# Hybrid decoder layer on one core: a first block in another order, square sums in one bank, the first state-space weights in steps, and stores issued by ScalarE

## The chip, the core and the metric

The kernel runs on one NeuronCore of a Trainium2 chip. The time is the device time of one execution in microseconds (us). The core has a matrix engine (TensorE, PE in the profile), VectorE (DVE), ScalarE (ACT), GpSimd (POOL) and SyncE (SP). Each engine works off its own list of instructions in order. SP and ACT also issue the DMAs of their queues, in their place in that list.

## The reference

One decoder layer for 2048 positions of width 1024, all in fp32:

```python
h = rmsnorm(x, norm_w)
u, z_s, q, k, v, z_a = split(h @ w_in, 6)            # 512 columns each
y_s = s5_branch(u, ...) * silu(z_s)                  # state space: 32 groups of 16 channels, a scan over positions
y_a = diff_attention(q, k, v, ...) * silu(z_a)       # 4 heads, two 64-wide maps each, causal
x = x + concat(y_s, y_a) @ w_out
x = x + sigmoid(x @ ple_w_gate) * (p @ ple_w_proj)
```

`rmsnorm` divides each row of x by the root of its mean square. The kernel multiplies x by the weights first and applies that factor to the result, so it needs a sum of squares for each position, but not before the products.

## The kernel before, in words

Every fp32 product is made of three matmuls of rounded parts: high x high, high x low, low x high (`xh`, `xl` of x, `wh`, `wl` of the weights). For each loaded chunk ACT makes the high part and DVE the low part.

**Phase 1**, to about 697 us, is the input projection, with the state-space branch and its gate unit as background work. The 2048 positions are 8 units of 256. The projection has 12 blocks: a half of the positions (4 units) times one of the six groups of 512 columns. Block 0 is u of the second half, block 1 u of the first half; then come k, s, v, q, a of the first half and s, k, v, q, a of the second. A block needs 8 weight chunks (k = 0 to 7); `ws` keeps 8 of them, and a chunk is released in the block's last unit and then replaced by that of the next block. Three raw chunks (`wraw`) can be in flight; ACT's queue loads them. `xs` keeps five units of x, which SP's queue loads.

In block 0 the first two units are computed together (L760): for k = 0 to 7, 12 matmuls for unit 0 and 12 for unit 1, into eight PSUM banks (4 `pmm`, 3 `pss`, 1 `ptr`). The other units of the u blocks are matmuls of line L781, the k, v, q, a blocks of L827. `stg` takes the u results out of PSUM (L791 by DVE, L793 by ACT).

`squares(unit)` (L253, L254) sums the squares of a unit over the partitions by two matmuls with a column of ones and brings the two columns from the bank `ptr` into `rstd` with one DVE instruction. The pool of `ptr` has one buffer, so the next unit's matmuls wait until that instruction is done. `norm(hf)` raises the eight columns of a half to the power -0.5 on POOL (L259), transposes them on PE (L262) and copies them out of PSUM twice by DVE (L264, L265).

The background is a generator, `ssm()`, that the projection loop advances by some steps after each unit. It makes rotary tables (L323 to L331: positions, angles, sine and cosine), the sum `ld` for attention's lambda from four small vectors `lv` (L335, L339), and the state-space parameters. For each four channel groups, `four(q4)` then makes weights: `na` (L539 to L543), matmuls for a residue (L574), `rs` (L577), which goes through memory and comes back as `M` (L578, L582), transposes (L585) into `wa`, and tables `tx`. `four` is itself a generator of four steps; for the first four groups it is run through at once. The loop over the 32 groups multiplies each group's input `U` by `wa` and by `mg` (made of `M`), scans on DVE, and writes `ysb` (L655) to memory (L656).

**Phase 2**, to about 1186 us, is attention with half of the output projection as filler; **phase 3** is the rest. The change touches neither.

The code is a program whose order on each engine is chosen by a scheduler: it takes instructions by priority (their place in the program, shifted for background work) as their inputs become ready in its own estimate. An edit therefore also moves instructions that it does not name.

Of the kernel before, what the change touches and what calls it, by code (L numbers as in the profile page):

```python
# [11 lines left out]
F32 = mybir.dt.float32  # L12
F32R = mybir.dt.float32r
I32 = mybir.dt.int32
AF = mybir.ActivationFunctionType
ALU = mybir.AluOpType
# [3 lines left out]
D = 1024  # L20
# [4 lines left out]
L = 8  # L25
NCH = S // L
H = 4
EPS = 1e-6
# [50 lines left out]
FLAG = 0  # L79
SADV = 400  # L80
SPB = dict(U=2, wa=2, wc=1, mg=1, xa=1)
FILL = [2] * 4 + [1] * 28
# [36 lines left out]
def hymba_kernel(ctx, tc, x_t, p_t, positions, norm_w, w_in, lam_re, lam_im, log_dt, b_re, b_im,  # L119
                 c_re, c_im, ssm_d, glu_w, glu_b, q_norm_w, k_norm_w, lq1, lk1, lq2, lk2,  # L120
                 subln_w, w_out, w_proj, w_gate, out):
    nc = tc.nc
    V, A, G, T = nc.vector, nc.scalar, nc.gpsimd, nc.tensor
# [74 lines left out]
    with ExitStack() as p1:  # L198
# [18 lines left out]
        sums = {}  # L217

        def build_xt(unit, first, whole):
# [27 lines left out]
            return make  # L247

        def squares(unit):

            pp = ps_tr.tile([128, 4, 128], F32, name="ptr")
            for j in range(2):
                T.matmul(pp[:, 0, j:j + 1], lhsT=sums[unit][:, j * 128:j * 128 + 128], rhs=ones, start=True, stop=True)  # L253
            V.tensor_scalar(rstd[:, unit * 2:unit * 2 + 2], pp[:, 0, 0:2], 1.0 / D, EPS, op0=ALU.mult, op1=ALU.add)  # L254

        def norm(hf):

            rs = rstd[:, hf * 8:hf * 8 + 8]
            G.tensor_tensor(rs, rs, negh[:, 0:8], op=ALU.pow)  # L259

            pp = ps_tr.tile([128, 4, 128], F32, name="ptr")
            T.transpose(pp[:8, 0, :], rs, ident)  # L262
            rt = [pt.tile([128, 8, 2, 8], F32, name=n_, bufs=2)[:8].rearrange("a b c d -> a (b c d)") for n_ in ("ra", "rb")]
            V.tensor_copy(rt[0], pp[:8, 0, :])  # L264
            V.tensor_copy(rt[1].rearrange("a (l c) -> a l c", l=L), pp[:8, 0, :].rearrange("a (c l) -> a l c", l=L))  # L265
            nc.sync.dma_start(rs_scr[hf].rearrange("(a q) -> a q", q=128), rt[0])
            nc.sync.dma_start(rl_scr[:, hf * 128:hf * 128 + 128].rearrange("l (a c) -> a l c", c=16),
                              rt[1].rearrange("a (l c) -> a l c", l=L))
# [36 lines left out]
        ws.fill()  # L305
        xs.fill()
        early_ctx.__exit__(None, None, None)
        early = None

# [3 lines left out]
        def ssm():  # L313

            with tc.tile_pool(name="p1s", bufs=1) as sp:
# [4 lines left out]
                pos_i = sp.tile([128, 16], I32, name="pos_i")  # L320
                nc.sync.dma_start(pos_i, positions)
                posT = sp.tile([128, 16], F32, name="posT")
                V.tensor_copy(posT, pos_i)  # L323
# [8 lines left out]

                lv = [sp.tile([128, 64], F32, name=f"lv{i}") for i in range(4)]
                for t_, a_ in zip(lv, (lq1, lk1, lq2, lk2)):
                    nc.sync.dma_start(t_, a_[0].partition_broadcast(128))  # L335
                ld = sp.tile([128, 2], F32, name="ld")
# [32 lines left out]
            with tc.tile_pool(name="ssA", bufs=1) as sp:  # L369
# [51 lines left out]
                k = 1  # L421
# [90 lines left out]
            with tc.tile_pool(name="ssB", bufs=2) as sp:  # L512
# [96 lines left out]
                for _ in four(0, made):  # L609
                    pass  # L610
                mg4 = within(made[0][2])
# [3 lines left out]
                for g in range(NG):  # L615
# [35 lines left out]
                    def behind(g=g, py=py, w=[w_[:, gs] for w_ in wc4], xa=xa):  # L651
# [3 lines left out]
                        A.copy(ysb, py)  # L655
                        nc.sync.dma_start(yg_scr[g].rearrange("l p c -> (l p) c"), ysb)  # L656
                        if g % 8 == 7:
# [81 lines left out]
        for bi, (hf, kind, c0) in enumerate(blocks):  # L739
            leaving = bi == len(blocks) - 1 or blocks[bi + 1][0] != hf  # L740
            for t in range(4):
# [5 lines left out]
                if kind in ("u", "zs"):  # L747
                    if kind == "u" and t == 0:
                        ude = [pg1.tile([128, L, 128], F32, name="stg") for _ in range(4)]
                    if bi == 0 and t < 2:  # L750

                        if t == 0:
                            first = [pool.tile([128, 512], F32, name=nm)[:, :256] for pool, nm, n in
                                     ((ps_mm, "pmm", 4), (ps_ss, "pss", 3), (ps_tr, "ptr", 1)) for _ in range(n)]
                            for k in range(8):
                                w = ws.get(k)
                                for t_ in range(2):
                                    for cb in range(4):
                                        for n, (a_, b_) in enumerate(passes):
                                            T.matmul(first[t_ * 4 + cb], lhsT=w[b_][:, cb * 128:cb * 128 + 128],  # L760
                                                     rhs=xs.get(t_)[a_][:, k, :],
                                                     start=(k == 0 and n == 0), stop=(k == 7 and n == 2))
                        pos_ = first[t * 4:t * 4 + 4]
# [53 lines left out]
                else:  # L817
# [3 lines left out]
                    for j in range(2):  # L821
# [10 lines left out]
                        if kind == "v":  # L832
                            vo = pt.tile([128, 512], F32, name="t2")
                            A.activation(vo, pm, AF.Copy, scale=rstd[:, ti:ti + 1])
                            nc.sync.dma_start(v_scr[rows, :], vo)
                        elif kind == "za":
# [35 lines left out]
                    if kind in ("q", "k"):  # L872
                        hi_s, lo_s = (qh_scr, ql_scr) if kind == "q" else (kh_scr, kl_scr)
                        nc.sync.dma_start(hi_s[:, :, tok:tok + 256].rearrange("h q t -> q h t"), sh_.bitcast(F32))
                        nc.sync.dma_start(lo_s[:, :, tok:tok + 256].rearrange("h q t -> q h t"), sl_.bitcast(F32))
                if kind == "u" and (bi, t) != (1, 3):
                    squares(xseq[xi + t])
                    if last_t:
                        norm(hf)
                if leaving:  # L880
                    xs.release()
# [517 lines left out]
```

## Time and profile before

| | |
|---|---|
| median of three runs | 1454.8 us (1452.43 to 1457.49) |
| the profiled execution | 1451.3 us |
| its span, first to last instruction | 1449.6 us |
| PE busy | 1383.4 us, 95% |
| DVE, ACT, POOL busy | 74%, 53%, 36% |
| mean granted TensorE clock | 0.992 |

PE is busy nearly all the time, so what can be gained or lost is in its idle stretches and in stretches at a lower clock. The views below are read in that order: how much PE idles in each stretch, who ended each wait, and what the releasing engine did before.

### The profile page before, as it was taken

Reading aid. Unit: us, or ns where it says so; the run is one execution under the profiler, and the core shown is the slowest. Engines: PE = TensorE matmul, PEld = TensorE weight load, DVE = VectorE, ACT = ScalarE, POOL = GpSimd, SP = SyncE. Lnnn points to the kernel's source line nnn. Section 1 sums busy time; section 2 is a strip of 40 time slices with the busy share of each in tenths; the row PEclk is TensorE's granted clock in tenths of the full one; section 3 lists DMA queues with packets and bytes.
Section 4 is the critical chain, followed back from the end, with each engine's and each line's share of the span. In section 5 each row is a group of like instructions: output and inputs, shape, how many; then the busy total and the mean of one; then the engine's idle time right before and its main releaser. Section 6 shows DMA issues by size and latency. Waiting matters only on the chain.

```text
span 1449.6 us, 27391 instructions
## 1 busy us (share of the span) xinstructions
PE 1383.4 (95%) x9602; PEld 1270.7 (88%) x9602; DVE 1066.3 (74%) x2527; ACT 767.9 (53%) x1689; POOL 521.3 (36%) x670
## 2 busy tenths in 40 slices
PE   7899899899999999999899999999998999999998
PEld 7898798778798888887699899989898999999998
DVE  8588898799798866675577867777877448666754
ACT  8443345456554555453586777767787523322231
POOL 6632500144000421331144454454434335543440
PEclk9999999999999999999999999999999999999999
DMA  7549756546765386556864653655434365132221
GB/s 248 152 109 293 209 178 191 166 145 191 245 192 165 107 240 186 138 150 203 240 176 121 164 143 117 162 149 142 127 88 161 138 231 227 59 117 81 73 74 59
DMA packets 219410, 230.34 MB, mean 159 GB/s; under 512 B 62712, under 2 KB 168328, under 8 KB 216712
## 3 DMA queue, kind: packets, MB, share of 16 engines
q1 hardware_dynamic: 203144, 199.22, 45.8%
q10 hardware_dynamic: 16128, 29.37, 6.6%
q8 instruction: 75, 1.23, 0.4%
q14 instruction: 63, 0.52, 0.1%
HBM read 152.19 MB, written 84.72 MB: 163 GB/s over the span
## 4 chain that ended last, share of the span: by engine, by line
PE 37%; DVE 5%; ACT 3%; issue 2%; DMA 2%; POOL 1%; SPq 0%; DVEq 0%; ACTq 0%; POOLq 0%
PE pg L1265 11%; PE po L1102 7%; PE pmf L931 6%; PE pss L1066 6%; PE pl L1281 3%; PE ptw L1098 3%; ACT s L1077 2%; DVE wgt L1157 1%; DVE s L1068 1%; PE pm L931 1%; DVE s L1090 1%; DMA wgr<-in_ple_w_gate_dram 1%; DVE wg L1153 0%; DMA yt_scr<-yo 0%; DMA yin<-yt_scr 0%
## 5 line engine op out<-in xcount | busy, mean ns | idle before, releaser
L827 PE MATMUL pmm<-wh,xh 128*128 128x512 f32 x512 | 198.3, 396 | 3.9 <-ACT wh L282 2.8
L827 PE MATMUL pmm<-wl,xh 128*128 128x512 f32 x512 | 200.4, 395 | 0.0
L827 PE MATMUL pmm<-wh,xl 128*128 128x512 f32 x512 | 200.0, 393 | 0.0
L1066 PE MATMUL pss<-ks,qd 128*128 128x512 f32 (+3 forms) x640 | 185.8, 388 | 10.3 <-DVE st L1068 6.3
L1077 ACT ACTIVATE s<-s,st 128x1024 f32<-128x1024 f32 (+4 forms) x192 | 171.7, 899 | 37.9 <-DVE st L1068 33.1
L1265 PE MATMUL pg<-oph,wg 128*128 128x256 f32 x896 | 164.4, 286 | 3.0 <-ACT oph L1238 2.9
L1102 PE MATMUL po<-vt,wt 128*128 128x128 f32 x1088 | 152.7, 276 | 0.8 <-ACT yo L1114 0.7
L1102 PEld LDWEIGHTS po<-vt,wt 128*128 128x128 f32 x1088 | 142.2, 192 | 7.2 <-ACT yo L1114 0.9
L1265 PEld LDWEIGHTS pg<-oph,wg 128*128 128x128 f32 x896 | 141.5, 195 | 3.4 <-ACT oph L1238 3.4
L1068 DVE CUSTOM_DVE_ANT_0 s<-pss,mk,st 128x512 f32<-128x512 f32 (+2 forms) x192 | 121.7, 652 | 24.3 <-PE pss L1066 22.9
L781 PE MATMUL pmm<-xh,wl 128*128 128x256 f32 x448 | 127.2, 287 | 2.7 <-DVE wl L283 2.6
L1265 PE MATMUL pg<-opl,wg 128*128 128x256 f32 x448 | 127.2, 285 | 1.2 <-POOL opl L1239 1.2
L781 PE MATMUL pmm<-xh,wh 128*128 128x256 f32 x448 | 123.0, 288 | 5.3 <-DVE stg L791 1.5
L781 PE MATMUL pmm<-xl,wh 128*128 128x256 f32 x448 | 125.8, 284 | 0.0
L1066 PEld LDWEIGHTS pss<-ks,qd 128*128 128x128 f32 x640 | 100.4, 192 | 22.8 <-DVE st L1068 11.6
L827 PEld LDWEIGHTS pmm<-wh,xh 128*128 128x128 f32 x512 | 96.1, 188 | 25.3 <-ACT wh L282 5.7
L827 PEld LDWEIGHTS pmm<-wl,xh 128*128 128x128 f32 x512 | 96.5, 188 | 19.2 <-DVE wl L283 1.5
L827 PEld LDWEIGHTS pmm<-wh,xl 128*128 128x128 f32 x512 | 96.5, 189 | 18.6
L931 PE MATMUL pmf<-yh,woh 128*128 128x256 f32 x352 | 104.8, 298 | 4.7 <-DVE x L1188 3.8
L1068 DVE CUSTOM_DVE_ANT_0 s<-pss,mk 128x512 f32<-128x512 f32 (+3 forms) x128 | 78.6, 630 | 34.3 <-PE pss L1066 28.6
L931 PE MATMUL pmf<-yh,wol 128*128 128x256 f32 x352 | 99.8, 284 | 0.0
L931 PE MATMUL pmf<-yl,woh 128*128 128x256 f32 x352 | 99.6, 283 | 0.0
(385 smaller groups left out, 3822.6 us busy)
## 6 DMA issues: line engine op xcount, KB each, us to landing
wraw<-in_w_in_dram ACTq DMA_DIRECT2D x96, 256.0 KB
xraw<-in_x_t_dram SPq DMA_DIRECT2D x40, 256.0 KB
tab<-tab_scr SPq DMA_DIRECT2D x64, 136.0 KB
qd<-qh_scr SPq DMA_DIRECT2D x64, 128.0 KB
qd<-ql_scr SPq DMA_DIRECT2D x64, 128.0 KB
xr<-in_x_t_dram SPq DMA_DIRECT2D x32, 256.0 KB
yin<-yt_scr SPq DMA_DIRECT2D x16, 512.0 KB
xp_scr<-xp SPq DMA_DIRECT2D x32, 256.0 KB
```

The lines of the kernel that those rows point to most:

```text
L781: T.matmul(pm, lhsT=w[b_][:, cb * 128:cb * 128 + 128], rhs=xt[a_][:, k, :], start=(k == 0 and n == 0), stop=(k == 7 and n == 2))
L827: T.matmul(pm, lhsT=xt[a_][:, k, j * 128:j * 128 + 128], rhs=w[b_], start=(k == 0 and n == 0), stop=(k == 7 and n == 2))
L931: T.matmul(pm[:, e, :], lhsT=w[k][b_][:, ms], rhs=y[a_][:, k, :], start=(k == 0 and n == 0), stop=(k == 3 and n == 2))
L1066: T.matmul(pss[:, :cl], lhsT=qd[:, e, m, tq], rhs=ks[m][:, c0:c0 + cl], start=e == 0, stop=e == 1)
L1068: V.tensor_tensor_reduce(sr[m][pi][:, o:o + cl], pss[:, :cl], mk[:, end - cl:end], scale=1.0, scalar=3.4e38 if ci == 0 else st[:, 2 * ci - ...
L1077: A.activation(sr[m][pi][:, :cl], sr[m][pi][:, :cl], AF.Exp, bias=st[:, ci + m:ci + m + 1], scale=-1.0, accum_out=st[:, 12 + 2 * pi + m:13 ...
L1090: V.scalar_tensor_tensor(s0, s1, st[:, 11:12], s0, op0=ALU.mult, op1=ALU.add)
L1098: T.transpose(ptw[:, k, :], blocks_[kg + k], ident)
L1102: T.matmul(po[:, 0:128], lhsT=wt[:, k, :], rhs=vt[:, kg + k, :], start=kg + k == 0, stop=kg + k == len(blocks_) - 1)
L1157: V.tensor_tensor(t_, a_, b_, op=ALU.subtract)
L1265: T.matmul(banks[mp][:, e], lhsT=wg[n][k][b_][:, m * 128:m * 128 + 128], rhs=x_[a_][:, k], start=k == 0 and q == 0, stop=k == 3 and q == 2)
L1281: T.matmul(banks[mp][:, e], lhsT=wp[k][b_][:, m * 128:m * 128 + 128], rhs=p_[a_][:, k], start=(k == 0 and q == 0), stop=(k == 1 and q == 2))
```

## The change

There are four edits, and one that goes with each of two.

1. In block 0 the second unit runs two steps behind the first (`UL = 2`): unit 0 with k = 0, 1, then unit 0 with k and unit 1 with k - 2, and at the end unit 1 with k = 6, 7. The third unit's loads are written after the second unit, those of the next two after the third.
2. The square sums of the four units of a half go to one bank, two columns each, with no evacuation between them. `norm` takes all eight columns at once with an ACT copy that scales, adds the epsilon on POOL, and copies the transposed columns out with ACT instead of DVE. The sums of block 0's first two units are written together after its second unit.
3. The first `four` gives a step back to the projection loop after each of its parts, like the later ones. The four loads of `lv` stand ahead of the rotary tables.
4. The stores of `ysb`, of v, and of the high parts of q and k are issued by ACT's queue instead of SP's: 32 + 16 + 16 DMAs.

```diff
@@ squares, norm
+        psq = [None, None]
         def squares(unit):
-            pp = ps_tr.tile([128, 4, 128], F32, name="ptr")
+            hf, u = divmod(unit, 4)
+            if psq[hf] is None:
+                psq[hf] = ps_tr.tile([128, 4, 128], F32, name="ptr")
             for j in range(2):
-                T.matmul(pp[:, 0, j:j + 1], lhsT=sums[unit][:, j * 128:j * 128 + 128], rhs=ones, start=True, stop=True)
-            V.tensor_scalar(rstd[:, unit * 2:unit * 2 + 2], pp[:, 0, 0:2], 1.0 / D, EPS, op0=ALU.mult, op1=ALU.add)
+                T.matmul(psq[hf][:, 0, u * 2 + j:u * 2 + j + 1], lhsT=sums[unit][:, j * 128:j * 128 + 128], rhs=ones,
+                         start=True, stop=True)
         def norm(hf):
             rs = rstd[:, hf * 8:hf * 8 + 8]
+            A.activation(rs, psq[hf][:, 0, 0:8], AF.Copy, scale=1.0 / D)
+            G.tensor_scalar(rs, rs, EPS, None, op0=ALU.add)
             G.tensor_tensor(rs, rs, negh[:, 0:8], op=ALU.pow)
...
-            V.tensor_copy(rt[0], pp[:8, 0, :])
-            V.tensor_copy(rt[1].rearrange("a (l c) -> a l c", l=L), pp[:8, 0, :].rearrange("a (c l) -> a l c", l=L))
+            A.copy(rt[0], pp[:8, 0, :])
+            A.copy(rt[1].rearrange("a (l c) -> a l c", l=L), pp[:8, 0, :].rearrange("a (c l) -> a l c", l=L))
@@ the background's first steps
+                for t_, a_ in zip(lv, (lq1, lk1, lq2, lk2)):
+                    nc.sync.dma_start(t_, a_[0].partition_broadcast(128))
                 posT = sp.tile([128, 16], F32, name="posT")
...
                 for _ in four(0, made):
-                    pass
+                    yield
@@ stores
-                        nc.sync.dma_start(yg_scr[g].rearrange("l p c -> (l p) c"), ysb)
+                        nc.scalar.dma_start(yg_scr[g].rearrange("l p c -> (l p) c"), ysb)
...
-                            nc.sync.dma_start(v_scr[rows, :], vo)
+                            nc.scalar.dma_start(v_scr[rows, :], vo)
...
-                        nc.sync.dma_start(hi_s[:, :, tok:tok + 256].rearrange("h q t -> q h t"), sh_.bitcast(F32))
+                        nc.scalar.dma_start(hi_s[:, :, tok:tok + 256].rearrange("h q t -> q h t"), sh_.bitcast(F32))
@@ block 0
-                            for k in range(8):
+                            for t_, k in [(t_, k_ - UL * t_) for k_ in range(8 + UL) for t_ in range(2) if 0 <= k_ - UL * t_ < 8]:
                                 w = ws.get(k)
...
-                if kind == "u" and (bi, t) != (1, 3):
-                    squares(xseq[xi + t])
+                if kind == "u" and (bi, t) not in ((0, 0), (1, 3)):
+                    for t_ in ((0, 1) if (bi, t) == (0, 1) else (t,)):
+                        squares(xseq[xi + t_])
                     if last_t:
                         norm(hf)
+                if bi == 0 and t == 1:
+                    xs.make(1)
+                if bi == 0 and t == 2:
+                    xs.fill()
```

**The order on PE, in block 1.** These are PE's rows in the first half's u block where square sums stand; `ptr_` is a bank's allocation and `acc_` a unit's sums. Before:

```order
L781 MATMUL pmm_1045<-xh_404,wl_974 128x256
L781 MATMUL pmm_1045<-xl_405,wh_973 128x256
L253 MATMUL ptr_1146<-ones_188,acc_411 128x1 x2
L253 MATMUL ptr_1339<-ones_188,acc_654 128x1 x2
L781 MATMUL pmm_1042<-xh_404,wh_985 128x256
```

and now:

```order
L785 MATMUL pmm_1040<-xl_613,wh_993 128x256
L258 MATMUL ptr_1141<-ones_188,acc_619 128x1 x2
L258 MATMUL ptr_1141<-ones_188,acc_649 128x1 x2
L258 MATMUL ptr_1141<-ones_188,acc_688 128x1 x2
L785 MATMUL pmm_1231<-xh_642,wh_908 128x256
```

Before, the second pair of sums needs a new allocation of the one bank; now three units stand in the same allocation.

**The order on DVE, at the start of block 1.** `wl` are the low parts of block 1's weights; `rpk`, `rpr`, `rpc` are the rotary angles, `xl` parts of later units of x. Before:

```order
L283 SCALAR_TENSOR_TENSOR wl<-wraw,nw,wh 128x512
L171 SCALAR_TENSOR_TENSOR rpr<-rpk,rpr 128x128
L283 SCALAR_TENSOR_TENSOR wl<-wraw,nw,wh 128x512
L172 SCALAR_TENSOR_TENSOR rpr<-rpk,rpr 128x128
L173 TENSOR_SCALAR rpr<-rpr 128x128
L174 SCALAR_TENSOR_TENSOR rpc<-rpr 128x128
L791 COPY stg<-pmm 128x32x8
L175 TENSOR_SCALAR rpc<-rpc 128x128
L254 TENSOR_SCALAR rstd<-ptr 128x2
L224 TENSOR_TENSOR xl<-xraw,xh 128x512
L283 SCALAR_TENSOR_TENSOR wl<-wraw,nw,wh 128x512 x2
```

and now:

```order
L225 TENSOR_TENSOR xl<-xraw,xh 128x512 x3
L795 COPY stg<-pmm 128x32x8
L290 SCALAR_TENSOR_TENSOR wl<-wraw,nw,wh 128x512 x3
L795 COPY stg<-pmm 128x32x8
L290 SCALAR_TENSOR_TENSOR wl<-wraw,nw,wh 128x512 x5
L795 COPY stg<-pmm 128x32x8 x2
L330 CAST posT<-pos_i 128x16
L333 TENSOR_SCALAR ang<-posT 128x16 x8
```

The eight weight chunks now stand together, and the angles come behind them.

**The order on DVE, at the start of the state-space loop.** From the first weights `na` to the residue `rs`, in the change from block 2 to block 3. Before:

```order
L543 TENSOR_TENSOR na<-na,tabt 128x512
L871 SCALAR_TENSOR_TENSOR stg<-ptr,knw,stg 128x4x128
L560 TENSOR_TENSOR tabt<-pt_2055 128x544
L853 TENSOR_TENSOR t_2417<-pmm,qst 128x512
L283 SCALAR_TENSOR_TENSOR wl<-wraw,nw,wh 128x512
L525 TENSOR_TENSOR Ul<-U,Uh 128x256
L847 TENSOR_REDUCE qst<-t_2564 128x8
L562 TENSOR_TENSOR tx<-tx,tabt 128x544
L283 SCALAR_TENSOR_TENSOR wl<-wraw,nw,wh 128x512
...
L560 TENSOR_TENSOR tabt<-pt_2055 128x544
L577 TENSOR_TENSOR rs<-pss,dd 128x64
```

and now:

```order
L547 TENSOR_TENSOR na<-na,tabt 128x512
L865 TENSOR_TENSOR ra<-t_2430,kc 128x128
L866 TENSOR_TENSOR rb<-t_2430,ks 128x128
L290 SCALAR_TENSOR_TENSOR wl<-wraw,nw,wh 128x512
L529 TENSOR_TENSOR Ul<-U,Uh 128x256
L564 TENSOR_TENSOR tabt<-pt_2045 128x544
L867 TENSOR_TENSOR t_2430<-ra,rb 128x8x8
L868 TENSOR_TENSOR t_2430<-ra,rb 128x8x8
L875 SCALAR_TENSOR_TENSOR stg<-ptr,knw,stg 128x4x128
L566 TENSOR_TENSOR tx<-tx,tabt 128x544
L581 TENSOR_TENSOR rs<-pss,dd 128x64
```

There were 12 instructions between the two and are 9, and the piece now starts when all but the last of block 3's weight chunks are done, where it stood ahead of all of them.

## Rows read from the trace of the kernel before

**Rows 1.** Busy time by stretch; columns: engines, PEclk the granted clock, DMA share.

```profile
core 0: us, PE busy (x) PEld busy (x) DVE busy (x) ACT busy (x) POOL busy (x), PEclk, DMA share, GB/s
0.00:200.00 200.00, 179.59 (x1269) 167.96 (x1270) 158.93 (x499) 96.02 (x181) 86.99 (x103) 0.99 0.67 202
200.00:700.00 500.00, 480.17 (x2730) 413.49 (x2729) 384.37 (x870) 256.44 (x565) 106.92 (x125) 1.00 0.61 179
700.00:1450.00 750.00, 723.61 (x5607) 689.29 (x5606) 523.01 (x1160) 415.46 (x944) 327.39 (x442) 0.99 0.43 134
```

**Rows 2.** Waits of PE in 0 to 200 us: total us, times, longest.

```profile
PE pmm L760 <- ACT xh L223: 6.1, 1, 6.1
PE ptr L253 <- DVE rstd L254: 3.5, 1, 3.5
PE pmm L781 <- DVE wl L283: 2.6, 3, 1.1
PE pss L530 <- ACT mgh L524: 1.9, 1, 1.9
PE pmm L781 <- DVE stg L791: 1.5, 1, 1.5
PE pmm L781 <- ACT wh L282: 1.3, 2, 0.9
...
PE pmm L781 <- DVE rpc L175: 1.0, 1, 1.0
PE pss L530 <- ACT wah L524: 0.6, 1, 0.6
```

**Rows 3.** PE's timeline at the end of L760: start, us, instruction, idle before.

```profile
30.76 0.28 PE L760 MATMUL ptr<-xl,wh 128*128 128x256 f32 x1
32.52 0.35 PE L781 MATMUL pmm<-xh,wh 128*128 128x256 f32 x1 [1.48 <-DVE stg L791]
32.71 0.28 PE L781 MATMUL pmm<-xh,wl 128*128 128x256 f32 x1
32.83 0.28 PE L781 MATMUL pmm<-xl,wh 128*128 128x256 f32 x1
```

**Rows 4.** DVE's timeline: the third weight chunk's low part; ahead of the square sums' wait.

```profile
8.30 0.74 DVE L283 SCALAR_TENSOR_TENSOR wl<-wraw,nw,wh 128x512 fp32r<-128x512 f32 x1
...
73.32 0.23 DVE L339 CUSTOM_DVE_ANT_0 lj<-lv,lv 128x64 f32<-128x64 f32 x1 [1.74 <-DMA lv<-in_lambda_k_dram]
...
73.55 0.15 DVE L254 TENSOR_SCALAR rstd<-ptr 128x2 f32<-128x2 f32 x1
```

**Rows 5.** Busy time by stretch, short stretches; columns as in Rows 1.

```profile
56.00:66.00 10.00, 7.33 (x57) 6.62 (x56) 7.12 (x15) 7.27 (x14) 4.83 (x5) 1.00 0.82 234
74.68:78.10 3.42, 3.42 (x19) 3.42 (x18) 2.66 (x5) 1.51 (x4) 3.42 (x5) 0.50 0.72 196
78.10:82.00 3.90, 3.90 (x34) 3.90 (x34) 3.27 (x14) 2.89 (x6) 2.96 (x4) 1.00 0.49 124
160.00:186.00 26.00, 20.32 (x148) 17.92 (x147) 25.46 (x51) 12.98 (x22) 12.35 (x13) 1.00 0.79 235
```

**Rows 6.** POOL's timeline: the power of the first half normalised.

```profile
61.82 1.66 POOL L259 TENSOR_TENSOR rstd<-rstd,negh 128x8 f32<-128x8 f32 x1 [1.43 <-DVE rstd L254]
```

**Rows 7.** PE's timeline at the first residue matmuls.

```profile
160.59 0.51 PE L574 MATMUL pss<-parg,na 128*128 128x16 f32 x4
```

**Rows 8.** The tile `rs`: its instruction, duration ns, first and last start us.

```profile
L577 DVE TENSOR_TENSOR rs<-pss,dd x1: 220/220/220, 167.1 to 167.1; 128x64 f32<-128x64 f32 x1
```

**Rows 9.** The tile `M` in 160 to 180 us, and who waited for it.

```profile
L582 SPq DMA_DIRECT2D M<-r_scr x1: 370/370/370, 172.9 to 172.9; - x1
L524 ACT CAST mgh<-M x1: 617/617/617, 177.7 to 177.7; 128x512 fp32r<-128x512 f32 x1
```

**Rows 10.** A store that ACT issues already: ns min/median/max, first and last start.

```profile
L842 ACTq DMA_DIRECT2D za_scr<-t x16: 326/326/352, 364.4 to 714.0; - x16
```

**Rows 11.** Waits of SP's queue: total us, times, longest.

```profile
SPq L656 <- ACT ysb L655: 20.2, 14, 4.9
```

**Rows 12.** Waits of PE in 200 to 700 us.

```profile
PE pss L530 <- ACT ysb L655: 3.2, 3, 2.6
...
PE pmm L827 <- ACT wh L282: 2.8, 4, 1.4
```

**Rows 13.** Waits of ACT.

```profile
ACT wh L282 <- DMA wraw<-in_w_in_dram: 47.9, 28, 5.8
```

More of the change, by code (lines that the diff above doesn't have):

```diff
@@ L80 @@
 SADV = 400
+UL = 2
 SPB = dict(U=2, wa=2, wc=1, mg=1, xa=1)
@@ L321, in ssm @@
                 nc.sync.dma_start(pos_i, positions)
+                lv = [sp.tile([128, 64], F32, name=f"lv{i}") for i in range(4)]
+                for t_, a_ in zip(lv, (lq1, lk1, lq2, lk2)):
+                    nc.sync.dma_start(t_, a_[0].partition_broadcast(128))
                 posT = sp.tile([128, 16], F32, name="posT")
@@ L331, in ssm @@
                 A.activation(cos_t, c, AF.Sin)
-                lv = [sp.tile([128, 64], F32, name=f"lv{i}") for i in range(4)]
-                for t_, a_ in zip(lv, (lq1, lk1, lq2, lk2)):
-                    nc.sync.dma_start(t_, a_[0].partition_broadcast(128))
                 ld = sp.tile([128, 2], F32, name="ld")
@@ L754, in hymba_kernel @@
                                      ((ps_mm, "pmm", 4), (ps_ss, "pss", 3), (ps_tr, "ptr", 1)) for _ in range(n)]
-                            for k in range(8):
+                            for t_, k in [(t_, k_ - UL * t_) for k_ in range(8 + UL) for t_ in range(2) if 0 <= k_ - UL * t_ < 8]:
                                 w = ws.get(k)
[L757 to L762, printed above, removed]
+                                for cb in range(4):
+                                    for n, (a_, b_) in enumerate(passes):
+                                        T.matmul(first[t_ * 4 + cb], lhsT=w[b_][:, cb * 128:cb * 128 + 128],
+                                                 rhs=xs.get(t_)[a_][:, k, :],
+                                                 start=(k == 0 and n == 0), stop=(k == 7 and n == 2))
                         pos_ = first[t * 4:t * 4 + 4]
@@ L873, in hymba_kernel @@
                         hi_s, lo_s = (qh_scr, ql_scr) if kind == "q" else (kh_scr, kl_scr)
-                        nc.sync.dma_start(hi_s[:, :, tok:tok + 256].rearrange("h q t -> q h t"), sh_.bitcast(F32))
+                        nc.scalar.dma_start(hi_s[:, :, tok:tok + 256].rearrange("h q t -> q h t"), sh_.bitcast(F32))
                         nc.sync.dma_start(lo_s[:, :, tok:tok + 256].rearrange("h q t -> q h t"), sl_.bitcast(F32))
-                if kind == "u" and (bi, t) != (1, 3):
-                    squares(xseq[xi + t])
+                if kind == "u" and (bi, t) not in ((0, 0), (1, 3)):
+                    for t_ in ((0, 1) if (bi, t) == (0, 1) else (t,)):
+                        squares(xseq[xi + t_])
                     if last_t:
                         norm(hf)
+                if bi == 0 and t == 1:
+                    xs.make(1)
+                if bi == 0 and t == 2:
+                    xs.fill()
+                    early_ctx.__exit__(None, None, None)
+                    early = None
                 if leaving:
```

3 lines of the change are left out of this document (removed).

## Prediction

> **What bounds the kernel now.** I read the views in this order: how much PE idles in each stretch, who ended those waits, what the releasing engine did just before, and where PE ran at the lower clock.
>
> PE is the bound nearly everywhere. It idles 20.4 us in the first 200 us, 19.8 in the next 500 and 26.4 in the rest [rows 1], so 1383.4 us of the span are matmuls that the change neither adds to nor takes away. What it can win lies in those gaps. The rest after 700 us is not touched, and of the first 200 us a start of 6.1 us is fixed, because the same first x part ends it before and after [rows 2]. What is left there is 14 us, and the reader should see in [rows 2] how it is split: 3.5 us behind the square sums, 2.6 behind low parts of weights, 1.9 and 0.6 behind the first state-space weights, 1.5 behind `stg`, 1.3 behind high parts, 1.0 behind a rotary angle. Each edit aims at one of these. The profiled execution took 1451.3 us, 3.5 below the median of the runs, so I work against 1451.3 and add 3.5 at the end.
>
> **(a) The first block.** Before, all eight banks of L760 are finished together, and the first matmul of L781 waits 1.48 us for the first `stg` [rows 3]. Now unit 0 ends 24 matmuls ahead of unit 1, 2.9 us at the pace of 0.12 us [rows 3]. That covers the 1.48 us: I take +1.5. The price could be at the other end: the third weight chunk is needed after 24 matmuls instead of 48. From PE's start at 6.1 that is not before 9.0, and its low part is done at 9.04 [rows 4], so nothing to a few hundredths is lost there; were every later chunk late by as much as the order moves it, 2.9 us would go. Bounds -1.4 to +1.5.
>
> **(b) The square sums.** PE waits 3.5 us for `rstd` [rows 2]. DVE's evacuation of the two columns starts at 73.55, directly behind the sum `lj`, which waited 1.74 us for the DMA of `lv` [rows 4]. The evacuation itself lasts 0.15, and it is what stands ahead of it on DVE that costs. With one bank there is no evacuation between units: PE has the three pairs in one run in the order, and the wait has no place left. The four `lv` loads, now ahead of the tables, remove the second cause as well. +3.5.
>
> Behind this wait the granted clock is 0.50, that is 1.2 GHz, from 74.68 to 78.10, and 19 matmuls start in that time. In the next 3.90 us, at 1.00, 34 do, 0.115 us each [rows 5]. At that pace 19 take 2.2 us, so the low clock cost 1.2 us. It fell right behind PE's 3.5 us pause, and the waits of about 1 us left it alone (56 to 66 us: 2.7 us idle in three pieces, granted 1.00 [rows 5]). Without the pause it should stay up: +1.2. The Trainium skill ("TensorE: Matmul & The Clock Gate", Terms) prices such a stretch at its length times the missing share of the clock, which here is an estimate of 1.7 us; the sum would be 0.5 higher by it. I keep 1.2, from matmuls counted at either level. Bounds of (b): 0, if another wait of that length takes its place (a rival below), to +4.7.
>
> **(c) Weights at the change to block 1.** In 56 to 66 us PE idles 2.7 us [rows 5], behind a low part, a high part and an angle (all within the sums of [rows 2]). On DVE the eight low parts now stand in one run, and the angles come after them. The angle's 1.0 goes entirely, since those instructions are moved out of the stretch. The low part's wait should go too; a high part that is late because its load is late stays late (DMA share there is 0.82 [rows 5]). I take +2.0; bounds 0 to +2.7.
>
> **(d) The norm chain.** Instead of one power per half behind finished `rstd`, the chain is ACT copy, POOL add, POOL power, transpose. The power takes 1.66 us [rows 6]; the trace has no such copy or add, so I bound each by 0 and 1.66 and get 1.7 to 5.0 for the three. By the order PE has 49 matmuls (5.9 us at 0.12) between the last sums and the transposes in the first half, and 39 (4.7 us) in the second. So it is covered unless the copy queues on ACT behind a wait for a load: those are 47.9 us in 28 waits, mean 1.7, longest 5.8 [rows 13]. A mean one gives 3.4 to 6.7 against 5.9 and 4.7: I take -0.5; bounds 0 and -4.7, the pause and low clock of (b) again. The DVE copies of the transposed columns go to ACT with nobody waiting closely, 0.
>
> **(e) The first state-space weights.** From the residue matmuls at 160.59 [rows 7] to `rs` at 167.1 [rows 8] and `mgh` done at 178.3 [rows 9] is a chain of 17.7 us. Meanwhile the order gives PE 63 projection matmuls and 16 transposes, and PE idles 5.7 us while DVE is busy 25.5 of 26 [rows 5]. So these took about 12.0 us, 7.2 in the matmuls at 0.115 and 0.3 for each transpose. After, 80 matmuls and 12 transposes stand there: 9.2 + 3.6 = 12.8. The chain has 9 DVE instructions instead of 12 in its first 6.5 us, so three times 0.54 = 1.6 less: 16.1. Idle 3.3 instead of 5.7, a gain of 2.4. But what remains now gathers at one place: the low parts that had let PE wait in small pieces are done before the piece starts, and PE runs up to the first state-space matmul earlier than `mgh` is there. Taking the transposes at twice a matmul, 0.23, PE has 12.0 us, idle is 4.1, a gain of 1.6; one pause of about 4 us, as long as that of (b), can bring back the low clock, -1.2. I take +1.0. Bounds: all 5.7, if the steps spread out cover the chain; and if the chain stays 17.7 with only the 9.2 us of matmuls beside it, 8.5 idle, -2.8. The whole branch begins about 10 us later in PE's order, but it ends well ahead of the end of phase 1 and is background there: 0.
>
> **(f) The stores.** 64 stores go from SP's queue to ACT's. ACT issues one in 0.326 us [rows 10], 21 us in all, on an engine that is busy half of the time. SP waited 20.2 us for `ysb` [rows 11]; nobody stood behind most of it. PE waits 3.2 us for `ysb` and 2.8 for high parts between 200 and 700 us [rows 12]. If a load on SP stood behind a waiting store it now comes sooner, up to +3.2; if weight loads stand behind stores on ACT, as much is lost. Here is a rule against the edit: "DMA: Bandwidth & Descriptors" of the Trainium skill (Issuing engines are not separate DMA queues) says that all issuers share the 16 engines and that issuing from several saves only the issue time. No row here tests it; by it this term would be zero at best. I take 0; bounds -3.2 to +3.2 and a lower one in a rival.
>
> Sum: 1.5 + 4.7 + 2.0 - 0.5 + 1.0 + 0 = 8.7. 1451.3 - 8.7 = 1442.6; with 3.5 for the median 1446.
>
> **Rivals.**
>
> *Everything gains.* (c) is 2.7, (e) 5.7, (f) 3.2, (d) 0: 17.8 us, median 1437. For it speaks that each wait has its cause moved; against it that DMA is busy 0.67 of the first 200 us [rows 1], so loads remain late.
>
> *The gain is paid back at the start of the state-space loop.* PE gets there earlier, and the chain over memory (`rs`, `M`, `mgh`, 11.2 us [rows 8, 9]) is not shorter: (e) at -2.8 with -1.2 of low clock replaces +1.0, and (d) at -1.2: 8.7 - 5.0 - 0.7 = 3.0, median 1452. For it: DVE is full there [rows 5].
>
> *The change doesn't do what it says in the square sums.* The wait moves to the transposes: the copy behind a late load on ACT, (d) -4.7, and (c) at 0 since the cause is the loads: 8.7 - 4.2 - 2.0 = 2.5, median 1452. Against it are the 49 matmuls of cover.
>
> *Slower: stores hold back weight loads.* A store of q or k is 512 KB, 2.2 us at the 235 GB/s of a full stretch [rows 5]. At six block starts (those around k, v and q in both halves) it can now stand ahead of the next block's weight loads in ACT's queue, and ACT already waits 47.9 us for these loads [rows 13]. One store's time per block start costs 13 us against 8.7: median 1459. It decides from 2.2 us of lateness at each: (8.7 + 4.4) / 6, with 4.4 the 0.3% that a measurement can tell from no change. Against it: the loads wait for released chunks as well as for the queue, and PE's waits for high parts are only 2.8 us so far [rows 12].
>
> **How the numbers follow.** Forecast 0.52, everything gains 0.18, paid back 0.16, moved wait 0.05, slower 0.09. Faster by over 0.3% (below 1450.4) is the first two, 0.70; the two at 1452 are within, 0.21; slower (above 1459.2) 0.09. The predicted time is 1446. Below, the range goes to 1437, the likely upper gain. Above, it goes to 1456, past the two at 1452 by the 3.5 us that a run may lie beside its median, and leaves out the slower case and some of each tail. The forecast alone is 1441 to 1450, from (e) and (f).
>
> **What would show it.** (a) no gap at the first L781. (b) no wait behind square sums, and granted 1.00 around 75 us. (c) idle in 56 to 66 us under 1. (d) the transposes of `norm` do not wait for POOL. (e) one wait of 3 to 5 us for `mgh` or `wah` at the first state-space matmul; two would be the paid-back case. (f) PE's waits for `wh` in 200 to 700 us stay at about 3 us; 10 or more would make the prediction wrong on the slow side, and idle in phase 1 down by more than 12 us on the fast side.

## The result, and the profile after

The change takes 1464.25 us (median of 4 runs, 1463.15 to 1466.97) where the kernel before takes 1453.62 in the same group of runs: a ratio of 1.0074, 95% interval 1.0051 to 1.0097. It is 10.6 us slower; I had forecast 1446, and 1437 to 1456 as the range. The profiled execution took 1464.1 us with a span of 1462.4. Later groups of runs were on several chips, on which the kernel before took 1453 to 1459 us; each ratio below is against the kernel before of the same group.

The busy time by stretch, in the columns of [rows 1], shows the same split as there:

```profile
0.00:200.00 200.00, 184.20 (x1317) 173.37 (x1318) 160.67 (x483) 94.44 (x183) 87.19 (x105) 0.99 0.65 204
200.00:700.00 500.00, 475.62 (x2674) 407.92 (x2673) 385.15 (x873) 259.09 (x566) 113.41 (x125) 0.99 0.60 179
700.00:1450.00 750.00, 724.19 (x5566) 691.44 (x5565) 519.59 (x1154) 415.27 (x942) 326.85 (x442) 0.98 0.42 133
```

PE's idle time fell from 20.4 to 15.8 us in the first 200 us, but rose from 19.8 to 24.4 in the next 500. The third row hides its loss: phase 3 begins later, so a stretch of dense work after 1450 us is no longer in it. A better measure is the time between two matmuls that both kernels have. These are the first and last starts of three lines on PE: the projection of the k, v, q, a blocks, attention's scores, and the products of phase 3. Of the kernel before:

```profile
L827 PE MATMUL pmm<-wh,xh x512: 387/389/628, 114.2 to 704.3; 128*128 128x512 f32 x171
L1066 PE MATMUL pss<-ks,qd x640: 222/393/688, 683.9 to 1136.7; 128*128 128x512 f32 x100, 128*128 128x256 f32 x28, 128*128 128x384 f32 x28, 128*128 128x128 f32 x4
L1265 PE MATMUL pg<-oph,wg x896: 280/283/580, 1231.4 to 1442.7; 128*128 128x256 f32 x180
```

and of the change, whose lines stand 4 and 11 further down:

```profile
L831 PE MATMUL pmm<-wh,xh x512: 387/389/763, 106.6 to 706.7; 128*128 128x512 f32 x171
L1077 PE MATMUL pss<-ks,qd x640: 220/393/776, 682.3 to 1144.2; 128*128 128x512 f32 x100, 128*128 128x384 f32 x28, 128*128 128x256 f32 x27, 128*128 128x128 f32 x5
L1276 PE MATMUL pg<-oph,wg x896: 278/283/553, 1243.7 to 1455.8; 128*128 128x256 f32 x180
```

Read them as three clocks. Block 2 starts 7.6 us earlier (106.6 for 114.2). At the end of phase 1 nothing is left of that: the last projection matmul is 2.4 us later, the first score matmul 1.6 earlier. Then the piece from the first score to the first matmul of phase 3, which I call the attention span, takes 561.4 us instead of 547.5. That is 13.9 us more, in a part of the program of which no line was edited. The windows of that span, first of the kernel before, then of the change:

```profile
683.90:1231.40 547.50, 528.05 (x3947) 491.66 (x3946) 394.40 (x1033) 361.42 (x878) 243.85 (x410) 0.99 0.53 160
682.30:1243.70 561.40, 536.76 (x3970) 501.28 (x3968) 395.05 (x1034) 363.90 (x880) 243.89 (x411) 0.98 0.51 157
```

Idle time of PE is 5.2 of the 13.9 us (24.64 for 19.45). The other 8.7 stand in PE's busy time. A part of them is a lower clock: in the change the granted clock is 0.50 from 901 to 908, 976 to 980 and 1113 to 1116 us, each time at a wait of PE of 1.5 to 3.8 us or just behind it. The kernel before has 1.00 from 717 to 1231 us.

PE's waits in the first 200 us, as in [rows 2], say how the early gain came about and where it went:

```profile
PE pmm L764 <- ACT xh L224: 5.5, 1, 5.5
PE pmm L831 <- DVE t L857: 3.9, 1, 3.9
PE pmm L785 <- ACT wh L289: 3.0, 2, 2.3
PE pss L534 <- ACT Uh L528: 2.1, 1, 2.1
PE pmm L785 <- ACT stg L797: 0.5, 1, 0.5
PE pmm L831 <- DVE wl L290: 0.3, 1, 0.3
PE ptr L258 <- DVE qnw L359: 0.3, 1, 0.3
```

The wait of the square sums is 0.3 instead of 3.5. The waits for `stg` ahead of the third unit and for the rotary angle are gone; the 0.5 for `stg` is another wait, at 80 us in block 1. New is the second row: 3.9 us in block 2, at 133 us, for DVE's `t` (L857; L853 before). In short stretches, with the columns of [rows 5], the clock stays up where it had fallen and falls at the new pause. First the change, then two of these stretches in the kernel before:

```profile
56.00:66.00 10.00, 9.27 (x75) 8.77 (x74) 4.13 (x6) 3.50 (x8) 9.13 (x11) 1.00 0.90 266
66.00:90.00 24.00, 23.50 (x193) 23.10 (x194) 13.65 (x49) 9.93 (x19) 9.92 (x13) 1.00 0.44 128
120.00:140.00 20.00, 16.10 (x66) 12.94 (x66) 15.04 (x86) 4.50 (x7) 6.02 (x8) 0.91 1.00 324
```

```profile
66.00:90.00 24.00, 20.53 (x159) 20.37 (x159) 15.95 (x51) 13.59 (x24) 14.44 (x17) 0.93 0.72 201
120.00:140.00 20.00, 19.02 (x84) 15.29 (x83) 17.53 (x95) 5.17 (x8) 4.01 (x5) 1.00 1.05 327
```

ACT's timeline just before that pause shows what is late:

```profile
126.78 0.64 ACT L470 COPY par<-s_bs 64x512 f32<-64x512 f32 x1 [5.98 <-DMA s_bs<-in_ssm_c_re_dram]
127.45 0.65 ACT L471 ACTIVATE par<-s_bs 64x512 f32<-64x512 f32 x1
128.12 0.65 ACT L472 ACTIVATE par<-s_bw 128x512 f32<-128x512 f32 x1
128.68 1.24 ACT L849 ACTIVATE t<-pmm,rstd 128x512 f32<-128x512 f32 x2
```

ACT stood 6 us for a load of the matrix C, and the squares of block 2's first products (L849) stood behind it in ACT's list. The reduction on DVE, the power on POOL and `t` on DVE follow them, and only `t` frees PE's bank. DMA is busy all of that stretch (share 1.00). PE had run ahead of the background work, and the background set the pace. The last matmul of block 2 starts at 158.1 us instead of 160.4, so 2.3 of the 7.6 us are left there.

### The profile page after: what moved, and what is told of

Its sections match the earlier page's. It is cut to its first block, busy times and chain, and to the rows that moved or that the text cites. A ratio compares the mean times of both kernels' runs of the same rounds, so it can differ in the third digit from the quotient of the medians.

```text
span 1462.4 us, 27302 instructions
## 1 busy us (share of the span) xinstructions
PE 1390.3 (95%) x9602; PEld 1278.8 (87%) x9602; DVE 1069.6 (73%) x2515; ACT 770.1 (53%) x1693; POOL 527.5 (36%) x672
## 4 chain that ended last, share of the span: by engine, by line
PE 53%; DMA 17%; DVE 14%; ACT 5%; POOL 5%; issue 4%; SPq 2%; ACTq 0%; DVEq 0%; POOLq 0%
PE pg L1276 11%; PE pmf L942 7%; PE po L1113 7%; PE pss L1077 6%; PE pmm L785 5%; PE pmm L831 4%; DMA wraw<-in_w_in_dram 3%; PE pl L1292 3%; PE ptw L1109 3%; PE pm L942 2%; POOL qst L853 1%; DMA gz<-zs_scr 1%; ACT s L1088 1%; DMA yin<-yt_scr 1%; DMA U<-ug_scr 1%
## 5 line engine op out<-in xcount | busy, mean ns | idle before, releaser
L831 PEld LDWEIGHTS pmm<-wh,xl 128*128 128x128 f32 x512 | 97.1, 190 | 18.2
```

The source lines that it names most:

```text
L831: T.matmul(pm, lhsT=xt[a_][:, k, j * 128:j * 128 + 128], rhs=w[b_], start=(k == 0 and n == 0), stop=(k == 7 and n == 2))
```

## The experiments

After the result I had four theories. **S**: stores on ACT hold back weight loads. **F**: the background, pushed back by four steps, is late. **O**: an edit lets the scheduler order everything behind it anew, phase 2 too, and that order costs the time. **D**: phase 2 loses because what phase 1 hands it comes late.

**Each edit undone alone.** The four kernels are the change with one of its four edits taken back.

```diff
# u_stores: yg_scr, v_scr and hi_s again
-  nc.scalar.dma_start(...)
+  nc.sync.dma_start(...)
# u_four (and the lv loads back behind the tables)
-  for _ in four(0, made): yield
+  for _ in four(0, made): pass
# u_sq: squares() and norm() of the kernel before
# u_blk: UL = 0, loads and sums of the first units as before
```

> The change without its fourth edit: all stores are issued by SP's queue as before. If stores ahead of weight loads in ACT's queue cost the 10 us (theory S), the time falls to that of before or below, 1447 to 1455 us, and the matmuls of the k, v, q, a blocks lose less on the way to the end of phase 1. If the loss is that the scheduler orders everything after an edit anew, phase 2 among it (theory O), the early gain of 6 us stays, the end of phase 1 moves by a few us either way, and phase 2 takes another time than with the change without any store of phase 1 being in it: total between 1445 and 1468.

> The change without its third edit: the first weights are made in one go, and the small vectors are loaded behind the tables, as before. If the background that is pushed back by four steps costs the time (theory F), the end of phase 1 comes 5 to 10 us earlier and the total falls to 1445 to 1455. By theory O the total is anywhere in 1445 to 1468 and phase 2's part of it changes too; by theory S it stays at 1464 within 3.

> The change without its second edit: square sums unit by unit through the one bank, evacuated by DVE. The wait of 3.5 us at the second unit and the low clock behind it may come back, so the early gain shrinks by up to 4.7. By theory O the total is anywhere in 1445 to 1468; by theories S and F it is 1464 to 1469.

> The change without its first edit: the first two units side by side. The gap of 1.5 us ahead of the third unit comes back. By theory O the total is anywhere in 1445 to 1468; by theories S and F it is 1464 to 1467.

Measured: `u_stores` 1.0060 (1.0036 to 1.0084), `u_four` 1.0064 (1.0039 to 1.0089), `u_blk` 1.0066 (1.0040 to 1.0091), `u_sq` 1.0134 (1.0091 to 1.0178). Taking back none of the edits brings the time back. Without the square sums' edit it looks worse still: beside the 1453.6 us of the first group it would be 1473, above what any of the theories allowed, though its interval reaches down to 1467 and so into O's range. S and F fall as they were put: neither the stores alone nor the steps alone are the cause. Each of the four kernels was also ordered anew, so these runs don't price the edits; `r_all_stores` below does that for the stores. The attention spans are 555.8, 560.5, 552.6 and 567.0 us: four other values, though all four kernels have the same code there.

**Phase 2's order exchanged.** Here and below a kernel is held to an order: after the program is written and before it is scheduled, each instruction of an engine gets an edge to the one ahead of it in the wanted list. The edge orders only; it adds no semaphore.

```diff
+ for p, i in pairs_in_the_wanted_order:
+     tc.add_manual_dep(i, p.name, NoSync)
```

`r_p2` is the change with phases 2 and 3 in the order of the kernel before, `x_p2` the kernel before with phases 2 and 3 in the order of the change.

> The change, with phase 2 and 3 held to the order that each engine has in the kernel before; phase 1 stands as in the change. Theory O (the scheduler's new order of phase 2 costs the 10 us lost there): 1464 falls to 1452 to 1457. Rival D (phase 2 loses because what phase 1 hands it comes late): it stays within 3 of 1464.

> The kernel before, with phase 2 and 3 held to the order that they have in the change. Theory O: 8 to 12 us slower than before, 1463 to 1468. Rival D: as before, 1453 to 1457.

Measured: `r_p2` 1.0026 (1.0006 to 1.0046), `x_p2` 1.0073 (1.0048 to 1.0098). The first matmul of scores and of phase 3, in `x_p2` and then in `r_p2`:

```profile
L1066 PE MATMUL pss<-ks,qd x640: 220/393/775, 687.1 to 1150.1; 128*128 128x512 f32 x100, 128*128 128x384 f32 x28, 128*128 128x256 f32 x27, 128*128 128x128 f32 x5
L1265 PE MATMUL pg<-oph,wg x896: 280/283/553, 1249.5 to 1460.6; 128*128 128x256 f32 x180
```

```profile
L1077 PE MATMUL pss<-ks,qd x640: 222/393/687, 695.9 to 1150.2; 128*128 128x512 f32 x100, 128*128 128x256 f32 x28, 128*128 128x384 f32 x28, 128*128 128x128 f32 x4
L1276 PE MATMUL pg<-oph,wg x896: 280/283/416, 1246.0 to 1457.7; 128*128 128x256 f32 x180
```

The attention span goes with the order, whatever stands ahead of it: 562.4 us for the kernel before with the change's order, 550.1 for the change with the order of before (561.4 and 547.5 in their own kernels). Put into the kernel before alone, the order costs 0.73%, 10.6 us, as much as the whole change. On this chip the kernel before took 1458.4 us, so the forecasts, which are times, are read as ratios. Beside the 1453.6 us of the first group `x_p2` would be at 1464.2, within O's range, and `r_p2` at 1457.4: 7 us below the change, where D allowed 3, and just above O's 1452 to 1457. D falls; for phase 2, O holds.

**The early gain in the order of before.** `r_b2_after` is the change with everything written from block 2 on in the order of before, `r_b2_e123` the same with the stores on SP.

> The change, with everything that is written from block 2 on held to the order of the kernel before (the 64 moved stores stand free in ACT's queue). Theory O: the early gain of about 6 us stays and nothing is lost behind it, 6 to 9 us faster than before, 1446 to 1450. Theory S (stores on ACT cost): 1455 or more, though the run without them below is fast. Rival D: 1460 or more.

> The same without the fourth edit: stores on SP's queue, and the order of the kernel before from block 2 on. Theory O: 6 to 9 us faster than before, 1446 to 1450. Against the run above it gives the fourth edit alone: within 3 us by my forecast of zero for it, 8 us or more by theory S.

Measured: 0.9998 (0.9976 to 1.0021) and 0.9987 (0.9967 to 1.0007). The loss is gone, as O says, but so is the gain, which O had kept. PE's timeline of `r_b2_e123` in block 2 tells where:

```profile
139.34 0.76 PE L831 MATMUL pmm<-wh,xh 128*128 128x512 f32 x1 [5.40 <-DVE s_er L417]
```

In `x_p2`, with phase 1 of the kernel before and in the same group of runs, PE waits 0.72 us at this place, until 140.0. Here it comes to block 2 some 5 us sooner (112.0 us against 117.1) and waits 5.4 us for DVE, which is no sooner: the wait ends at 139.3. By the last matmul of block 2 nothing of the 5 us is left (163.9 us here, 163.1 in `x_p2`).

**Taking that wait away.** In `r_b2_dve` all stays as in `r_b2_e123` but 12 rows of DVE; in `k_pool` all stays as in the change but three copies. `r_all_stores` is the kernel before in its own order with the fourth edit alone, and `a_again` the change once more.

```diff
# r_b2_dve: DVE's list, rows of block 2's first two products
-  place n      qst, t, ra, rb of products 1 and 2
+  place n - 27
# k_pool
-  A.copy(K1[0:64], bs[0:64]); A.mul(K1[64:128], bs[64:128], -1.0); A.mul(K2, bw, -1.0)
+  G.tensor_copy(...); G.tensor_scalar(..., -1.0, None, op0=ALU.mult) x2
```

> The change once more, beside the others of this group on one chip, as their yardstick: about 1.007 times the kernel before.

> The change, every engine held to the order that it has there, but the three copies that wait for the loads of the matrix C stand on POOL instead of ACT. In the change they make ACT stand from 120.8 to 126.8 us with the squares of block 2's first products behind them, and PE waits 3.9 us at 133. If that in-order wait on ACT is where the early gain goes, the wait at 133 falls to 1 us or less and the end of block 2 comes about 3 us earlier. Rival: DVE's chain of small instructions is as late, and the wait stays at 3 us or more. In the total at most 3 us, -0.2%, of the change.

> The run with edits 1 to 3 and the order of the kernel before from block 2 on, held to exactly its own order on every engine, with 12 DVE instructions of block 2's first two products (reduction, scaling, rotation) 27 places earlier, ahead of small instructions of the state-space parameters. There PE waited 5.4 us at 139 for them. If PE's early gain is only lost in that queue, the wait goes to under 1.5 us, and the time falls by 3 to 5 us to 0.995 to 0.997 of the kernel before. Rival: the parameters behind them are late instead, and PE loses it again at the first state-space matmuls (160 to 190 us): 0.998 to 1.000.

> The kernel before, all held to its own order, with the fourth edit alone: the 64 stores issued by ACT. My forecast for this edit: no change within 3 us. Theory S: 5 to 13 us slower by waits for high parts of the weights.

`a_again` gave 1.0072 (1.0041 to 1.0102), `k_pool` 1.0082 (1.0052 to 1.0112), `r_b2_dve` 1.0002 (0.9985 to 1.0019), `r_all_stores` 0.9996 (0.9976 to 1.0016).

The stores cost nothing, as forecast. In `k_pool` ACT's squares came at 124.39 us, 4.3 earlier, and yet PE waited 4.9 at that place. POOL's timeline says why:

```profile
128.26 0.67 POOL L470 COPY par<-s_bs 64x512 f32<-64x512 f32 x1 [23.61 <-DMA s_bw<-in_ssm_c_re_dram]
129.01 1.60 POOL L471 TENSOR_SCALAR par<-s_bs 64x512 f32<-64x512 f32 x1
130.70 1.55 POOL L472 TENSOR_SCALAR par<-s_bw 128x512 f32<-128x512 f32 x1
132.33 0.20 POOL L852 TENSOR_SCALAR qst<-qst 128x8 f32<-128x8 f32 x1
```

The copies wait for the same load on POOL, and the power that block 2's product needs stands behind them there. So my expectation missed: the wait moved to another list of the same chain.

`r_b2_dve` did what it should at its place, and the time did not follow. PE's timeline, first from block 2 to the first residue matmuls and then at the change to phase 2:

```profile
132.82 0.47 PE L831 MATMUL pmm<-wh,xh 128*128 128x512 f32 x1 [0.79 <-DVE s_er L417]
...
146.18 0.66 PE L872 MATMUL ptr<-ident,t 128*128 128x128 f32 x4 [2.08 <-DVE stg L875]
...
160.36 0.62 PE L578 MATMUL pss<-parg,na 128*128 128x16 f32 x4 [1.44 <-DVE na L547]
...
702.59 1.62 PE L1077 MATMUL pss<-ks,qd 128*128 128x512 f32 x3 [2.52 <-DMA qd<-qh_scr]
715.81 0.85 PE L1077 MATMUL pss<-ks,qd 128*128 128x384 f32 x2 [3.57 <-DVE st L1079]
```

the last two places in `r_b2_e123`:

```profile
703.93 0.94 PE L1077 MATMUL pss<-ks,qd 128*128 128x512 f32 x3 [0.35 <-DMA qd<-qh_scr]
715.87 1.01 PE L1077 MATMUL pss<-ks,qd 128*128 128x384 f32 x2 [2.76 <-DVE st L1079]
```

and the residue matmuls in `r_all_stores`, which ran in the same group on the same chip and, at 0.9996, can stand for the kernel before:

```profile
L575 PE MATMUL pss<-parg,na x64: 177/263/263, 161.1 to 443.9; 128*128 128x16 f32 x64
```

The wait of 5.4 us is 0.8. But block 2 starts 6.1 us sooner than in `r_all_stores` (109.1 for 115.2) and the first residue matmul only 0.7 (160.4 for 161.1): new waits of 2.1 us for `stg` and of 1.4 for the first weights `na` stand between. The second is what the rival in my expectation said: the parameters' instructions on DVE, now behind the 12, are late instead. The last residue matmul is 2.7 us sooner (441.2 for 443.9). At the end of phase 1 PE waits 2.5 us for the first loads of phase 2, where `r_b2_e123` waits 0.35, and these two are at 715.8 us side by side. Each of these is one profiled execution, and `r_b2_e123` ran on another chip, so the places are read, not shown; that the gain does not arrive is what the ratio shows.

**What in phase 2's order costs the time.** The filler's input is loaded as `yin`; ACT casts it to its high part `yh`, and POOL subtracts to get the low part `yl`. In the change ACT waits 14.4 us for these loads (six times), where the kernel before waits 6.4, and behind one of these casts PE waits 3.8 us for `yo`, attention's finished block, which ACT copies out of PSUM. Theory C: these waits in ACT's and POOL's lists are the cost. `p_cast`, `b_cast` and `best1` move five casts 8 places later on ACT and the subtractions behind them 7 places on POOL; `p_cast2` puts those subtractions behind a power chain (five small POOL instructions of attention that end in a power) instead of inside one.

```diff
# ACT's list in phase 2, five times
-  yh cast, then 8 rows of softmax work
+  8 rows of softmax work, then yh cast
# POOL's list
-  yl, then 7 rows
+  p_cast: 7 rows, then yl;  p_cast2: up to the end of a power chain, then yl
```

> The change, every engine held to its own order, but with five of the casts of the filler's input (ACT) 8 places later in phase 2 and the subtractions behind them (POOL) 7 places later. In the change ACT stands 3 to 4 us at each of three of them until the load lands, with the softmax work of attention behind it, though PE needs the filler's input 18 to 45 us later. If these in-order waits are what the order of phase 2 costs (theory C), PE's waits at about 902, 975 and 1017 us and the low clock behind them go, and the time falls by 5 to 10 us to 1.001 to 1.004 of the kernel before. Rival: the interleaving as a whole is worse, of which the casts are only a sign: 1.006 to 1.008 as without.

> The same move in the kernel before, held to its own order, where the casts wait 0 to 1.9 us. Theory C: at most 3 us to gain, 0.998 to 1.000. Rival: 1.000 or more.

> The move of the casts in the version with edits 1 to 3, the order of the kernel before from block 2 on and the 12 DVE instructions earlier. By theory C what the kernel before gains by the move, on top of that version's 1.000: 0.996 to 1.000. It is faster than both kernels if under 0.998.

> As the run before it with the casts 8 places later on ACT, but each subtraction on POOL stands right behind the end of a tile's power chain, not inside one (there DVE's ya, and PE behind it, waited 4.3 us for that chain). Theory C: the waits for yo and for ya both go, and the time is 1.001 to 1.004 of the kernel before. Rival, the interleaving as a whole: PE's idle time in 700 to 1130 us stays within 3 us of the change's, in other waits, and the time is 1.006 or more.

Measured: `p_cast` 1.0116 (1.0085 to 1.0147), `b_cast` 1.0024 (1.0011 to 1.0038), `best1` 1.0024 (1.0008 to 1.0041), `p_cast2` 1.0112 (1.0085 to 1.0138). None was faster than the kernel it came from, so I asked what the holding itself costs.

```diff
# a_self, b_self: the change and the kernel before, each held to its own order, nothing moved
```

> The change held to its own order on every engine, nothing moved: what holding an order costs by itself. If nothing, 1.007 times the kernel before, like the change; if as much as 1.011, the two runs with moved casts are no slower than their control and say nothing against theory C.

> The kernel before held to its own order, nothing moved: the control for all runs that hold its order. If holding costs nothing, 1.000; if it costs, the runs with edits 1 to 3 in the order of the kernel before (0.9987 and 1.0002) are gains against this one.

Measured: `a_self` 1.0107 (1.0077 to 1.0138), `b_self` 1.0000 (0.9986 to 1.0014). Holding costs nothing in the kernel before. In the change `a_self` lies above the change's 1.0072 to 1.0074, but their intervals overlap. The trace of `a_self` says where it is later:

```profile
L1077 PE MATMUL pss<-ks,qd x640: 220/393/774, 690.6 to 1152.8; 128*128 128x512 f32 x100, 128*128 128x384 f32 x28, 128*128 128x256 f32 x27, 128*128 128x128 f32 x5
L1276 PE MATMUL pg<-oph,wg x896: 276/283/415, 1252.9 to 1465.1; 128*128 128x256 f32 x180
```

Its attention span is 562.3 us, as in the change (561.4, and 563.3 in `a_again`). So, as far as one execution each can tell, holding costs nothing in phase 2, and what `x_p2` lost there is the order's. What `a_self` has more lies ahead of the first score matmul (690.6 us for 682.3 in the change); on the same chip the kernel before, held, is later there too (689.5 in `b_self` for 683.9). Over all runs that have one of the two orders in phase 2 and move nothing in it, the span goes by the order: 556.4 to 563.3 us in five with the change's order (the shortest is `k_pool`), 545.9 to 550.3 in seven with that of before.

Against `a_self` the moved casts gain nothing. I had put on record that a control at 1.011 would leave these two runs saying nothing against theory C by their ratios. What speaks against C is the span: 569.0 us in `p_cast` and 567.1 in `p_cast2`, not shorter than 562.3. PE's waits in 700 to 1130 us of the change, and then of `p_cast2`:

```profile
PE pss L1077 <- DVE st L1079: 4.9, 5, 2.1
PE po L1113 <- ACT yo L1125: 3.8, 1, 3.8
PE pss L1077 <- DMA qd<-qh_scr: 3.6, 2, 2.2
```

```profile
PE pss L1077 <- DVE st L1079: 7.6, 7, 2.4
PE pss L1077 <- DMA qd<-qh_scr: 6.4, 2, 4.9
PE pss L1077 <- DVE st L1093: 1.8, 1, 1.8
```

The wait for `yo` is gone, ACT's wait for `yin` too (0.7 us in all), and other waits have grown: PE idles 19.1 us in this stretch, in the change 18.2. Theory C falls for these five casts: they are a sign of this order and not its cost.

## Why the prediction was wrong

**The first steps held, nearly to the size.** (a) The third unit follows the second without a gap:

```profile
30.72 0.28 PE L764 MATMUL ptr<-xl,wh 128*128 128x256 f32 x1
30.84 0.28 PE L785 MATMUL pmm<-xh,wh 128*128 128x256 f32 x1
```

(b) The square sums' wait is 0.3, and the granted clock is 1.00 from 66 to 90 us. (c) Idle time in 56 to 66 us went from 2.7 to 0.7; I had taken 2.0 off. (d) `norm`'s transposes waited 0.2 us for POOL. I had put these at 1.5 + 4.7 + 2.0 - 0.5 = 7.7; block 2 starts 7.6 us earlier. That the two agree so closely is in part luck. The start, which I had called fixed, came 0.6 us sooner (5.5 for 6.1). The low clock of (b) had cost more than 1.2 us: the x in [rows 5] counts all matmuls that run in a stretch, and not 19 but 16 start in those 3.42 us, which take 1.9 at 0.12 each, so that 1.5 were lost. Small new waits, 0.5 for `stg` and 0.3 for `wl`, took back about as much.

**(e) was close in size, wrong in place.** At the start of the state-space loop PE waits in two pieces (2.3 for a high part at 168 us, 2.1 for `Uh` at 178) and not once for `mgh`. The first residue matmul is at 172.9 us instead of 160.59 [rows 7]: the loop starts 12 us later, where I had said 10, and `mgh` is no longer what PE waits for. By my own sign two waits were the paid-back case. The working also set the 5.7 us of idle time in a stretch of 26 us against a chain of 17.7; a wait of 0.5 at 185 us lies behind that chain.

**(f) held.** Alone, in an unchanged order, the edit gives 0.9996; the rival with 13 us fell. It was my one slower case (0.09, at 1459 us), so the right sign in it is luck: the stores did not act.

**The step that failed first** is the sentence "The rest after 700 us is not touched", behind the reading of [rows 1]. It is so of the code, and not of the program. The sum had no term for phase 2's order, and that term is 10.6 us by `x_p2` in the kernel before, and 0.48% (1.0074 less 1.0026), some 7 us, by `r_p2` in the change. I had listed the orders of both kernels side by side for the first 200 us and had taken attention's to be the same without doing so there.

**The second** is that I carried 7.7 us gained by 110 us to the end of the kernel. I had the rival "the gain is paid back", but put it at the state-space loop, with DVE's 25.5 of 26 us [rows 5] as its sign. In the change 5.3 of the 7.6 us are paid back 27 us earlier, in block 2. The reasons are read from the traces and not shown by a run of their own, and the trace of before could have told them: the products of that block go through ACT, DVE and POOL, which work off the background's parameters in the same lists, and DMA is busy throughout (share 1.05 in 120 to 140 us before, 1.00 after). In the order of before the gain came to nothing (0.9998 and 0.9987), and with the wait in block 2 taken away it still came to nothing (1.0002), with most of it gone by the first residue matmuls, where the rival had put it. A PE that idles 5% is not a bound whose every saved wait counts.

**What stays open.** Which rows of phase 2's new order cost the 10 us is not settled; the exchange shows that it is the order, and the casts were the only part tried. Phase 1 in the change's order may cost a little as well, 1.0026 in `r_p2` against 0.9998 in `r_b2_after`, with intervals that overlap. The traces don't settle it: with one and the same order of phase 1 the first score matmul comes at 682.3 to 695.9 us in the profiled executions of the change, `a_again`, `a_self` and `r_p2`. Why phase 1 of `a_self` is later than that of the change was not found. No version was clearly faster than the kernel before; the best is `r_b2_e123` with 0.9987, and its interval reaches over 1.

## What to carry to other kernels

Where a scheduler sets the order, compare the orders of the whole program and not of the edited part: an edit in the first tenth reordered all that follows, and that cost more than the edit gave. Hold everything but the edited part to its old order to measure an edit by itself; two such runs, the order exchanged both ways, told more here than four with one edit undone. And a wait removed early counts only if the next shared resource, an in-order list or a load, is also sooner: look for the next instruction that both the faster and the slower chain go through.

## What the runs showed that I had not expected

The order of phases 2 and 3 alone, with not an instruction more or less, is worth 0.7% of the time. The same kernel took 1453.2 us (20 runs) in one group and 1458.4 (26 runs) in another, 0.36% apart, so that terms of a few us are found only beside runs of the same group. And three small copies, 0.65 us each on ACT, took 0.67, 1.60 and 1.55 us on POOL.
